# Low weight parts kept in DRAM between two blocks, and GpSimd's subtractions halved

## The chip, the cores and the metric

The kernel runs on one core of a Trainium2 chip. The metric is the device time of one execution in microseconds. Before the change three runs gave a median of 2254.72 us (2252.18 to 2258.6). Engines are named as in the profile: PE is TensorE's matmul, PEld its weight load, DVE is VectorE, ACT is ScalarE, POOL is GpSimd, SP issues DMAs.

## The reference

One layer of a hybrid decoder over 1024 prompt tokens and 64 decoded tokens, model width 2048. Everything is float32.

```python
h = rms_norm(x, p['norm_g'])
proj = h @ p['w_in']                      # 2048 x 6784
ps, g_a, u_b, g_b, u_c, v_c, g_c = jnp.split(proj, SPLIT_IDX, axis=-1)
y_a, new_shift, new_wkv = rwkv7_mix(ps, ...)   # 16 heads of 64, delta-rule state
y_b, new_pool = pool_mix(u_b, ...)             # trailing windows 2/4/8/16
y_c, vn_c = chunk_gate(u_c, v_c, ...)          # 128-position chunks
cat = jnp.concatenate([y_a * silu(g_a), y_b * silu(g_b), y_c * silu(g_c)], axis=-1)
out = x + cat @ p['w_out']                # 2048 x 2048
y = rms_norm(out, final_norm_g)
```

The two large products are what the change is about: each needs its weights, and the kernel computes each in float32 quality from pieces of lower precision.

## The kernel before, in words

The tokens go through in two blocks: block 0 is 512 prompt tokens and the 64 decoded ones, block 1 the other 512. Each block runs an in-projection (53 column tiles of 128 columns, in the order of `ORDER`) and then an out-projection. Both blocks read the whole of `w_in` and `w_out`.

A weight piece is 128 x 512 floats (256 KB). It is loaded by SP into `raw` (`wload`), rounded by ACT to the matmul type float32r as `whi` (`whigh`), and what the rounding lost is `wlo` = `raw` - `whi` (`wlow`). That subtraction stands on POOL for three pieces out of four and on DVE for the fourth (`wcount`, `V[6]`=4). A column tile has four pieces; a dense step (`dense_k`) makes three products: `whi` with the high activations (L237), `whi` with the low ones (L240), `wlo` with the high ones (L243). So each of the 212 pieces of `w_in` is loaded, rounded and subtracted twice, once in each block.

`Feed` says when that happens: while piece c is multiplied, step 1 rounds piece c+3, step 3 loads piece c+6, and step 0 (the last) subtracts piece c+3. There are 4 `raw`, 5 `whi` and 5 `wlo` buffers, so `whi` and `wlo` of piece c+5 take the places of piece c's.

Between the dense products run the side computations of the RWKV branch (`rwkv_unit`, 16 units a block, two for a pair of heads). They are generators: each `yield` names a number of ticks, a tick passes after a dense step, and what a generator emits is put into the program there. All engines execute in the order of the program as it is written (a manual schedule), so a PE instruction of a unit whose operands are late stops the dense products behind it. The places to follow are: the products of queries and keys `gp` (L680), which read `KG` and `BE`; `KG` is made by POOL (L664, L666) and by DVE (L558, a helper that all scalar_tensor_tensor instructions of DVE share); before these stand DVE's `kp` (L644), reciprocals (L640) and `BE` (L647); the recurrence over chunks (`cp` L871, copy to `W` by DVE and ACT L875 and L876, `cp` L883, copies to `SV` L885, `cq` L892, next `SV` by L558); and the inverse, whose product `d` (L823) reads `Q` (L836). POOL carries the inverse of 16 x 16 blocks (`Tu` L779, `Xu` L780) and, for the decoded rows of block 0, `svx` (L918). The unit's small transfers (`ndr`, `Nu`, `Xu`, `xd`, `X`) go through the same SP queue as the weights.

Of the kernel before, what the change touches and what calls it, by code (L numbers as in the profile page):

```python
# [9 lines left out]
F32 = mybir.dt.float32  # L10
F32R = mybir.dt.float32r
# [43 lines left out]
def tile_trunk(  # L55
# [21 lines left out]

    def ctile(shape, name, dt=F32):
        return const.tile(shape, dt, name=name)

    # ---------------------------------------------------------------- constants
# [26 lines left out]
    # ---------------------------------------------------------------- normalised inputs  # L108
    # the operand of a block's products, high and low parts, four feature tiles each
# [34 lines left out]
    # ---------------------------------------------------------------- dense pieces  # L144
    wcount = [0]

    def wload(src):
        raw = wp.tile([P, BLK + ND], F32, tag="raw", name="raw", bufs=4)
        sync.dma_start(raw[:, :512].rearrange("p (k c) -> p k c", c=src.shape[2]), src)
        return raw  # L150
# [6 lines left out]
    def wlow(raw, whi, eng=None, keep=None):  # L157
        wlo = keep[1] if keep else wp.tile([P, 512], F32R, tag="wlo", name="wlo", bufs=5)
        wcount[0] += 1
        eng = eng or (pool_e if wcount[0] % V[6] else dve)  # L160
        eng.tensor_sub(wlo, raw[:, :512], whi.bitcast(F32))  # L161
        return wlo

    def out_plan(b):
        # column group, feature tile, token tiles
        if b == 1:
            return [(g, k, range(4)) for g in range(4) for k in range(NK)]
        return [(g, k, range(5)) for g in range(3) for k in range(NK)] + [(3, k, t) for t in (range(2), range(2, 5)) for k in range(NK)]
# [8 lines left out]
    class Feed:  # L177
        # the weights' pieces in their order: loads run ahead of the splits, and those ahead of the products
        def __init__(self):
            self.src = [x for b in range(2) for x in [(ct, kh) for ct in ORDER for kh in range(4)] + out_plan(b)]  # L180
            self.raws, self.his, self.parts, self.keep, self.i = {}, {}, {}, {}, 0

# [8 lines left out]

        def low(self, i, eng=None):
            self.high(i)
            if i in self.raws and i not in self.parts:
                self.parts[i] = self.his[i], wlow(self.raws[i], self.his[i], eng, self.keep.get(i))

        def piece(self, ls):
            i = self.i
            for j in range(i, i + ls):
                self.low(j)  # L200
            self.i += 1
            return self.parts[i]

        def ahead(self, step):
            if step == V[3] % 4:
                self.high(self.i - 1 + LS)
            if step == V[4] % 4:
                self.low(self.i - 1 + LS)
            if step == V[5] % 4:
                j = self.i - 1 + LS + LD  # L210
                if len(self.src[j - 1]) == 2 or len(self.src[j - 2]) == 3:
                    self.load(j)

    # generators that go on beside the products, in ticks of those
# [33 lines left out]
    def dense(b, ct, hi, lo, feed, part=None):  # L248
        # part: the first half, where it is there already
        assert feed.src[feed.i] == (ct, 0)  # L250
        spans = ((0, UN), (UN, BLK + ND)) if b == 0 else ((0, BLK),)
        ps = [part or psd_tile()] + [psd_tile() for _ in spans[1:]]
        todo = list(zip(spans, ps))[1 if part else 0:]
        steps = 0
        for kh in range(4):
            piece = feed.piece(LS)
            for (t0, t1), q in todo:
                for k in range(4 * kh, 4 * kh + 4):
                    dense_k(q, hi, lo, k, piece, t0, t1, b == 1)
                    steps += 1  # L260
                    if steps < NK * len(todo):
                        tick()
                    if steps % len(todo) == 0:
                        feed.ahead(steps // len(todo) % 4)
        if b == 0:
            return [ps[0][:, :UN], ps[1][:, :UN + ND]]
        return [ps[0][:, :UN], ps[0][:, UN:]]
# [4 lines left out]
    with tc.tile_pool(name="prep", bufs=2) as pp, tc.tile_pool(name="setup", bufs=1) as sp, tc.manual_schedule():  # L272
        # the gain's row, spread over the partitions by the tensor engine
# [86 lines left out]
        def rescale(tt):  # L360
            # the scale of a tile as a diagonal, which its transposition multiplies by
            d = pp.tile([P, P], F32, name=f"dg{tt}", bufs=1)
            dve.tensor_scalar(d, ident, ss5[tt], None, op0=ALU.mult)
            return d
# [174 lines left out]
    # ---------------------------------------------------------------- RWKV branch  # L539
    def shift_evac(wk, b, ct, ps, xs, u):  # L540
        # token shift of half a column tile: (1 - mu) * now + mu * before
# [20 lines left out]
    def rwkv_unit(wk, b, p, u, lora, lw, got, pair_ops, zk):  # L562
        # yields the steps of the dense products to let pass before it goes on
# [29 lines left out]
        # decay, in-context rate, squared key norms  # L593
# [66 lines left out]
        # phase operands of a chunk and head, in the rows of the head: keys and queries;  # L660
        # in the other head's rows: their products with the chunk's keys
# [12 lines left out]
        # within-chunk products, masked to the past  # L674
# [25 lines left out]
        # X = (I - N)^-1: diagonal blocks of 16 by substitution, then blocks of 32 and 64  # L700
# [45 lines left out]
        # per head: the states, then the corrections, in the rows of the head, and the values in the others  # L746
# [29 lines left out]
        for r in range(1, 15):  # L776
# [4 lines left out]
            if dec and r == 7:  # L781
                # states of the decoded sequences
# [72 lines left out]
        # chunk recurrence  # L855
# [7 lines left out]
        # chunks one after the other; the decoded rows beside the first  # L863
# [42 lines left out]
        # group norm (token-major), bonus and gate (feature-major)  # L906
# [67 lines left out]
    # ---------------------------------------------------------------- pooling branch  # L974
# [34 lines left out]
    # ---------------------------------------------------------------- in-projection of a block  # L1009
    def in_block(wk, b, hi, lo, feed, part, raws):  # L1010
# [28 lines left out]
        def start(ps):  # L1039
# [12 lines left out]
            # stationary operands of both heads of a pair; the blocks between the heads stay zero  # L1052
# [67 lines left out]
        # spatial gating  # L1120
# [73 lines left out]
        def states():  # L1194
            # states that leave
# [49 lines left out]
    # ---------------------------------------------------------------- out-projection of a block  # L1245
    def cat_load(b, k):
        raw = wp.tile([P, BLK + ND], F32, tag="raw", name="raw", bufs=4)
# [8 lines left out]
    def first_cats(b, hi, lo, raws):  # L1256
        # the first rows of the out-projection, as soon as the last column tile has read what they overwrite
# [10 lines left out]
    def out_block(op, b, hi, lo, feed, raws):  # L1268
# [12 lines left out]
        if b == 0:  # L1281
            # the decoded rows: high and low parts side by side, so that two passes carry all their products
# [37 lines left out]
        def next_rows(j):  # L1320
            # a quarter of the next block's normalised inputs, feature-major
# [42 lines left out]
        def close(g, tt, q):  # L1364
# [15 lines left out]
            # the norm of a row's end  # L1380
# [29 lines left out]
        # the tiles of a group begin and end one after the other  # L1410
# [73 lines left out]
```

## Time and profile before

| quantity | value |
|---|---|
| median of 3 runs | 2254.72 us |
| profiled execution, first to last instruction | 2252.0 us |
| PE busy | 2163.5 us (96%) |
| PEld busy | 1860.5 us (83%) |
| DVE busy | 1212.4 us (54%) |
| POOL busy | 1066.7 us (47%) |
| ACT busy | 1006.0 us (45%) |
| DMA, mean | 98 GB/s, 221.18 MB |

The page gives the profiled execution by its span alone, 2252.0 us, which lies 2.7 us under the median of the runs. The table is read from the top: one engine is nearly always at work, and all others are idle half of the time. Such a table says little about the others' worth: what counts is where PE stands still, for how long, and which engine's instruction ended that. The windows of the profile cut the span into its stages: 60 to 960 us is block 0's in-projection, 960 to 1245 its out-projection, 1245 to 2060 block 1's in-projection, and the rest block 1's out-projection.

### The profile page before, as it was taken

The numbers are of one execution on the slowest core, as the hardware profiler recorded it, in microseconds if no ns is written. First come the engines' busy times: TensorE is split into PE (matmuls) and PEld (weight loads), VectorE is DVE, ScalarE is ACT, GpSimd is POOL, SyncE is SP. The second block draws the span as 40 slices with busy tenths as digits, with TensorE's granted clock in tenths as the row PEclk, the third lists the DMA queues.
The fourth block names the chain that finished last, engine by engine and source line by source line (L and its number), as shares of the span: only waits on it lengthen the run. The fifth ranks groups of instructions, "written<-read, shape, count | busy, mean of one in ns | idle before, by whom it ended". The sixth has DMA issues, their size and how long they took to land. (4 is left out here: it accounts for less than half of the span.)

```text
span 2252.0 us, 40898 instructions
## 1 busy us (share of the span) xinstructions
PE 2163.5 (96%) x14706; PEld 1860.5 (83%) x14706; DVE 1212.4 (54%) x2978; ACT 1006.0 (45%) x2680; POOL 1066.7 (47%) x1820
## 2 busy tenths in 40 slices
PE   7999999999999999999999999999999999999998
PEld 6998988988889899998887777777777778887786
DVE  6477677567667523214236467767676753323313
ACT  5344554554555442223334445555556454222323
POOL 5455555554555534223335455655555463432332
PEclk9999999999999999999999999999999999999999
DMA  5232232322222233336545432222222233334634
GB/s 153 77 75 64 75 78 58 76 72 65 74 70 70 74 87 96 93 95 195 175 150 178 129 81 77 74 72 77 75 73 78 72 85 95 95 116 129 191 122 140
DMA packets 390306, 221.18 MB, mean 98 GB/s; under 512 B 124054, under 2 KB 355736, under 8 KB 389207
## 3 DMA queue, kind: packets, MB, share of 16 engines
q1 hardware_dynamic: 390104, 218.58, 34.0%
q8 instruction: 116, 1.90, 0.4%
q14 instruction: 86, 0.70, 0.1%
HBM read 191.90 MB, written 26.61 MB: 97 GB/s over the span
## 5 line engine op out<-in xcount | busy, mean ns | idle before, releaser
L237 PE MATMUL dps<-a,whi 128*128 128x256 f32 (+1 forms) x2544 | 883.6, 347 | 2.1 <-ACT whi L154 1.9
L243 PE MATMUL dps<-a,wlo 128*128 128x256 f32 (+1 forms) x2544 | 844.5, 332 | 1.1 <-POOL wlo L161 0.7
L240 PE MATMUL dps<-a,whi 128*128 128x256 f32 (+1 forms) x2544 | 843.0, 331 | 0.0
L161 POOL TENSOR_TENSOR wlo<-raw,whi 128x512 fp32r<-128x512 f32 x415 | 550.5, 1330 | 591.2 <-ACT whi L154 541.7
L237 PEld LDWEIGHTS dps<-a,whi 128*128 128x128 f32 x2544 | 484.7, 191 | 48.9 <-issue 10.2
L243 PEld LDWEIGHTS dps<-a,wlo 128*128 128x128 f32 x2544 | 484.1, 190 | 33.5 <-POOL wlo L161 1.1
L240 PEld LDWEIGHTS dps<-a,whi 128*128 128x128 f32 x2544 | 485.5, 191 | 26.0 <-issue 0.2
L154 ACT CAST whi<-raw 128x512 fp32r<-128x512 f32 x552 | 338.6, 620 | 351.9 <-PE dps L240 117.4
L161 DVE TENSOR_TENSOR wlo<-raw,whi 128x512 fp32r<-128x512 f32 x137 | 101.8, 743 | 164.3 <-ACT whi L154 163.7
L1360 PE MATMUL ops<-whi,a 128*128 128x512 f32 x448 | 176.6, 394 | 2.5 <-ACT a L1253 1.8
L1361 PE MATMUL ops<-wlo,a 128*128 128x512 f32 x448 | 176.8, 395 | 2.2 <-POOL wlo L161 1.7
L1362 PE MATMUL ops<-whi,a 128*128 128x512 f32 x448 | 175.1, 391 | 0.1
L779 POOL TENSOR_TENSOR Tu<-Xu,Nu 32x14 f32<-32x14 f32 (+9 forms) x448 | 127.0, 283 | 27.3
L780 POOL TENSOR_TENSOR Xu<-Xu,Tu 32x14 f32<-32x14 f32 (+9 forms) x448 | 120.6, 269 | 35.1
L1361 PEld LDWEIGHTS ops<-wlo,a 128*128 128x128 f32 x448 | 84.1, 188 | 23.8 <-POOL wlo L161 5.6
L1360 PEld LDWEIGHTS ops<-whi,a 128*128 128x128 f32 x448 | 84.1, 188 | 22.0 <-ACT a L1253 2.3
L898 ACT ACTIVATE ZD<-SV,DC 64x64 f32<-64x64 f32 x192 | 66.2, 345 | 79.9 <-DVE SV L558 77.2
L1362 PEld LDWEIGHTS ops<-whi,a 128*128 128x128 f32 x448 | 84.1, 188 | 19.5 <-DVE a L1254 1.8
L922 POOL TENSOR_TENSOR sv<-sv,neghalf 128x4 f32<-128x4 f32 (+1 forms) x32 | 37.1, 1158 | 132.8 <-DVE sv L921 116.5
L871 PEld LDWEIGHTS cp<-SV,KG 128*128 128x128 f32 x544 | 77.5, 190 | 24.6 <-DVE SV L558 19.8
L871 PE MATMUL cp<-SV,KG 128*128 128x64 f32 x544 | 81.4, 271 | 9.6 <-DVE SV L558 9.6
L892 PEld LDWEIGHTS cq<-SV,Q 128*128 128x128 f32 x544 | 76.4, 190 | 15.3 <-DVE SV L885 11.0
(318 smaller groups left out, 3103.2 us busy)
## 6 DMA issues: line engine op xcount, KB each, us to landing
raw<-in_w_in_dram SPq DMA_DIRECT2D x424, 256.0 KB
raw<-in_w_out_dram SPq DMA_DIRECT2D x144, 256.0 KB
raw<-cat SPq DMA_DIRECT2D x32, 256.0 KB
res<-in_x_prompt_dram SPq DMA_DIRECT2D x32, 256.0 KB
out_dram<-res SPq DMA_DIRECT2D x32, 256.0 KB
x<-in_x_prompt_dram SPq DMA_DIRECT2D x4, 1024.0 KB
x<-in_x_prompt_dram SPq DMA_DIRECT2D x6, 512.0 KB
ndr<-N SPq DMA_DIRECT2D x48, 64.0 KB
```

Source lines behind the costliest of these rows:

```text
L154: act_e.copy(whi, raw[:, :512])
L161: eng.tensor_sub(wlo, raw[:, :512], whi.bitcast(F32))
L237: pe.matmul(o, lhsT=wh, rhs=xh, start=(k == 0), stop=False)
L240: pe.matmul(o, lhsT=wh, rhs=xl, start=False, stop=False)
L243: pe.matmul(o, lhsT=wl, rhs=xh, start=False, stop=(k == NK - 1))
L779: pool_e.tensor_tensor(tv, bc(Xu[:U, 0:r, r], 2, e), bc(Nu[:U, r, r + 1:16], 1, r), op=ALU.mult)
L780: pool_e.tensor_tensor(Xu[:U, 0:r, r + 1:16], Xu[:U, 0:r, r + 1:16], tv, op=ALU.add)
L871: pe.matmul(cw[i][:, h], lhsT=KG[:, q, h].rearrange("p a t -> p (a t)"), rhs=SV[:, q, h, :], start=True, stop=True)
L892: pe.matmul(cz[i][:, h], lhsT=Q2[:, q, h].rearrange("p a t -> p (a t)"), rhs=SV[:, q, h, :], start=True, stop=True)
L1360: pe.matmul(q, lhsT=ah, rhs=whi, start=(k == 0), stop=False)
L1361: pe.matmul(q, lhsT=ah, rhs=wlo, start=False, stop=False)
L1362: pe.matmul(q, lhsT=al, rhs=whi, start=False, stop=(k == NK - 1))
```

## The change

Two things are changed in the weights' path. Block 0 stores each `wlo` of `w_in`'s pieces 8 to 211 into a DRAM tile `wld` when the piece's products begin, and block 1 loads it from there and makes no subtraction for it; its `raw` is still loaded and rounded. In block 1 the load of `wlo`, and with it the rounding, of piece c+4 stands at step 3 of piece c, where before the rounding of piece c+4 stood at step 1 of piece c+1. And each subtraction that POOL still has is two instructions of 128 x 256 instead of one of 128 x 512. The `raw` buffers lose 64 unused columns. All other hunks of the diff only take out comments.

```diff
+    wld = drp.tile([DIN // P * 4, P, 512], F32, name="wld")
...
     def wload(src):
-        raw = wp.tile([P, BLK + ND], F32, tag="raw", name="raw", bufs=4)
+        raw = wp.tile([P, BLK], F32, tag="raw", name="raw", bufs=4)
...
         eng = eng or (pool_e if wcount[0] % V[6] else dve)
-        eng.tensor_sub(wlo, raw[:, :512], whi.bitcast(F32))
+
+        for c in ([slice(q * 256, (q + 1) * 256) for q in range(2)] if eng is pool_e else [slice(0, 512)]):
+            eng.tensor_sub(wlo[:, c], raw[:, c], whi[:, c].bitcast(F32))
         return wlo
...
             self.raws, self.his, self.parts, self.keep, self.i = {}, {}, {}, {}, 0
+
+            self.nin = 4 * len(ORDER)
+            self.n1 = self.nin + len(out_plan(0))
...
+        def cached(self, i):
+            return self.n1 + 8 <= i < self.n1 + self.nin
+
         def low(self, i, eng=None):
             self.high(i)
             if i in self.raws and i not in self.parts:
-                self.parts[i] = self.his[i], wlow(self.raws[i], self.his[i], eng, self.keep.get(i))
+                if self.cached(i):
+                    wlo = wp.tile([P, 512], F32R, tag="wlo", name="wlo", bufs=5)
+                    sync.dma_start(wlo.bitcast(F32), wld[i - self.n1])
+                else:
+                    wlo = wlow(self.raws[i], self.his[i], eng, self.keep.get(i))
+                self.parts[i] = self.his[i], wlo
...
             self.i += 1
+            if self.cached(i + self.n1):
+                sync.dma_start(wld[i], self.parts[i][1].bitcast(F32))
             return self.parts[i]
...
             if step == V[5] % 4:
+                if self.cached(self.i + LS):
+                    self.low(self.i + LS)
                 j = self.i - 1 + LS + LD
```

PE's instructions and their order stay as they were. On POOL the subtractions leave block 1's in-projection. Its program at the end of a unit's inverse in block 1 (`Tu`, `Xu`) up to the next unit's `KG`, before:

```order
L779 TENSOR_TENSOR Tu<-Xu,Nu 32x14
L780 TENSOR_TENSOR Xu<-Xu,Tu 32x14
L161 TENSOR_TENSOR wlo<-raw,whi 128x512 x2
L664 TENSOR_TENSOR KG<-xr,D 64x4x64 x2
L161 TENSOR_TENSOR wlo<-raw,whi 128x512
L719 TENSOR_TENSOR kpl<-kp,kph 128x256
L922 TENSOR_TENSOR sv<-sv,neghalf 128x4
L161 TENSOR_TENSOR wlo<-raw,whi 128x512
```

and now (line numbers are higher in the changed file, by 4 at the subtraction and by 19 in the unit):

```order
L798 TENSOR_TENSOR Tu<-Xu,Nu 32x14
L799 TENSOR_TENSOR Xu<-Xu,Tu 32x14
L683 TENSOR_TENSOR KG<-xr,D 64x4x64 x2
L738 TENSOR_TENSOR kpl<-kp,kph 128x256
L941 TENSOR_TENSOR sv<-sv,neghalf 128x4
```

Four `wlo` are gone from that stretch, and `KG` follows the inverse at once. DVE loses its quarter of the subtractions in the same stage. On POOL in block 0, from the decay's copies of a unit to the decoded rows' `svx`, before:

```order
L633 COPY DC<-D 128x4
L636 COPY DCd<-D 128x8
L161 TENSOR_TENSOR wlo<-raw,whi 128x512 x2
L664 TENSOR_TENSOR KG<-xr,D 64x4x64
L666 TENSOR_TENSOR KG<-xr,D 64x64
L664 TENSOR_TENSOR KG<-xr,D 64x4x64
L666 TENSOR_TENSOR KG<-xr,D 64x64
L161 TENSOR_TENSOR wlo<-raw,whi 128x512
L918 TENSOR_TENSOR svx<-SV,bm_89 128x512 x2
```

and now:

```order
L652 COPY DC<-D 128x4
L655 COPY DCd<-D 128x8
L165 TENSOR_TENSOR wlo<-raw,whi 128x256 x4
L683 TENSOR_TENSOR KG<-xr,D 64x4x64
L685 TENSOR_TENSOR KG<-xr,D 64x64
L683 TENSOR_TENSOR KG<-xr,D 64x4x64
L685 TENSOR_TENSOR KG<-xr,D 64x64
L165 TENSOR_TENSOR wlo<-raw,whi 128x256 x2
L937 TENSOR_TENSOR svx<-SV,bm_90 128x512 x2
```

Nothing moved there; each subtraction has become two. On SP in block 1, around a unit's first small transfers (`X` back from DRAM, then `ndr`), before:

```order
L806 DMA xd_79<-Xu 32x16x16
L149 DMA raw<-in_w_in_dram 128x4x128
L810 DMA X<-xd_79 64x4x64 x2
L149 DMA raw<-in_w_in_dram 128x4x128 x2
L724 DMA ndr<-N 64x4x64 x2
L149 DMA raw<-in_w_in_dram 128x4x128
L744 DMA Nu<-ndr 32x16x16
```

and now:

```order
L825 DMA xd_79<-Xu 32x16x16
L207 DMA wlo<-wld 128x512
L151 DMA raw<-in_w_in_dram 128x4x128
L829 DMA X<-xd_79 64x4x64 x2
L207 DMA wlo<-wld 128x512
L151 DMA raw<-in_w_in_dram 128x4x128
L207 DMA wlo<-wld 128x512
L151 DMA raw<-in_w_in_dram 128x4x128
L743 DMA ndr<-N 64x4x64 x2
L207 DMA wlo<-wld 128x512
L151 DMA raw<-in_w_in_dram 128x4x128
L763 DMA Nu<-ndr 32x16x16
```

A load of `wlo` stands in front of every load of `raw`, and the unit's transfers keep their places among them.

## Rows read from the trace of the kernel before

**Rows 1.** Windows by stage: length, busy time by engine, clock, DMA share, GB/s.
```profile
60.00:960.00 900.00, 873.13 (x7422) 820.70 (x7421) 522.48 (x1421) 406.60 (x1168) 448.45 (x836) 0.98 0.28 75
960.00:1245.00 285.00, 281.52 (x1427) 237.02 (x1426) 113.44 (x148) 107.96 (x206) 103.89 (x89) 1.00 0.50 158
1245.00:2060.00 815.00, 780.60 (x4814) 618.02 (x4813) 482.74 (x1244) 394.55 (x1120) 416.15 (x776) 1.00 0.31 86
```

**Rows 2.** Waits of PE, block 1's in-projection: total us, times, longest.
```profile
PE gp L680 <- DVE KG L558: 12.9, 17, 3.0
PE cp L883 <- ACT yc L880: 7.0, 7, 1.1
PE cp L871 <- DVE SV L558: 5.2, 13, 0.4
```

**Rows 3.** Timeline of DVE near 1418 us: start, us, instruction.
```profile
1417.94 1.56 DVE L644 TENSOR_TENSOR kp<-kp,xk 128x256 f32<-128x256 f32 x1
...
1420.35 0.21 DVE L875 COPY W<-cp 64x64 f32<-64x64 f32 x1
```

**Rows 4.** Timeline of POOL, same stretch.
```profile
1417.94 1.28 POOL L161 TENSOR_TENSOR wlo<-raw,whi 128x512 fp32r<-128x512 f32 x1
```

**Rows 5.** Timeline of PE, same stretch; in brackets its idle time before.
```profile
1421.18 0.43 PE L883 MATMUL cp<-W,XB 128*128 128x64 f32 x2 [1.10 <-ACT yc L880]
```

**Rows 6.** Groups by line and shape, 1245 to 2060 us: busy us, mean ns, idle before.
```profile
L161 POOL TENSOR_TENSOR wlo<-raw,whi 128x512 fp32r<-128x512 f32 x157 | 206.2, 1316 | 151.6 <-ACT whi L154 138.1 <-PE mp L1101 4.1 <-DVE BE L558 3.8
...
L161 DVE TENSOR_TENSOR wlo<-raw,whi 128x512 fp32r<-128x512 f32 x52 | 41.5, 798 | 33.8 <-ACT whi L154 33.6
...
L644 DVE TENSOR_TENSOR kp<-kp,xk 128x256 f32<-128x256 f32 x16 | 15.2, 950 | 2.5 <-ACT kp L631 2.1
...
L719 POOL TENSOR_TENSOR kpl<-kp,kph 128x256 fp32r<-128x256 f32 x16 | 12.1, 754 | 23.5 <-ACT kph L716 22.9
...
L967 DVE TENSOR_TENSOR bv<-yf,bv 128x256 f32<-128x256 f32 x16 | 6.8, 426 | 36.6 <-ACT yf L963 36.6
```

**Rows 7.** Waits of PE, block 0's in-projection.
```profile
PE d L823 <- DVE Q L836: 8.9, 7, 1.4
PE cp L871 <- DVE SV L558: 4.3, 7, 0.8
PE cq L892 <- DVE SV L885: 3.8, 7, 0.6
```

**Rows 8.** Timeline of DVE near 380 us.
```profile
379.01 2.05 DVE L558 SCALAR_TENSOR_TENSOR BE<-xk,der,Di 64x320 f32<-64x320 f32 x2
...
381.35 1.88 DVE L558 SCALAR_TENSOR_TENSOR KG<-xk,der,D 64x256 f32<-64x256 f32 x2
```

**Rows 9.** Timeline of POOL, same stretch.
```profile
379.21 1.50 POOL L161 TENSOR_TENSOR wlo<-raw,whi 128x512 fp32r<-128x512 f32 x1 [0.99 <-POOL KG L666]
380.68 2.47 POOL L918 TENSOR_TENSOR svx<-SV,bm 128x512 f32<-128x512 f32 x2
```

**Rows 10.** Timeline of PE, same stretch.
```profile
381.37 0.68 PE L892 MATMUL cq<-SV,Q 128*128 128x64 f32 x4 [0.59 <-DVE SV L885]
383.49 0.65 PE L823 MATMUL d<-Q,X 64*64 64x32 f32 x16 [1.44 <-DVE Q L836]
```

**Rows 11.** Windows at a granted clock of 0.50, columns as in Rows 1.
```profile
299.25:302.66 3.41, 3.41 (x18) 2.65 (x16) 3.23 (x15) 1.66 (x6) 0.02 (x1) 0.50 0.00 0
384.58:388.00 3.42, 3.42 (x16) 3.27 (x15) 3.24 (x14) 0.74 (x3) 0.00 (x0) 0.50 0.02 5
...
736.16:742.98 6.82, 6.82 (x27) 4.10 (x28) 5.16 (x16) 1.34 (x3) 2.41 (x2) 0.50 0.10 23
1289.12:1292.53 3.41, 3.41 (x14) 2.25 (x13) 0.14 (x2) 1.51 (x4) 1.97 (x2) 0.50 0.00 0
```

**Rows 12.** Groups by line and shape, 60 to 960 us.
```profile
L161 POOL TENSOR_TENSOR wlo<-raw,whi 128x512 fp32r<-128x512 f32 x144 | 191.6, 1333 | 181.2 <-ACT whi L154 152.2 <-DVE BE L558 14.2 <-POOL KG L666 6.7
```

**Rows 13.** Waits of ACT, block 0's out-projection.
```profile
ACT whi L154 <- DMA raw<-in_w_out_dram: 27.6, 17, 4.8
```

More of the change, by code (lines that the diff above doesn't have):

```diff
@@ L1246, in cat_load @@
     def cat_load(b, k):
-        raw = wp.tile([P, BLK + ND], F32, tag="raw", name="raw", bufs=4)
+        raw = wp.tile([P, BLK], F32, tag="raw", name="raw", bufs=4)
         sync.dma_start(raw[:, :BLK], catd[b][k, :, :BLK])
```

## Prediction

> **What bounds the kernel now.** I read the windows by stage first [rows 1]. In block 0's in-projection PE is at work for 873.1 of 900 us, in block 1's for 780.6 of 815; the idle time is 26.9 and 34.4 us. In the out-projection between them it is 3.5 us. DVE and POOL are busy for about half of each stage. PE's instructions and their order are the same in both kernels, so the change can give no more than PE's idle time and what a low clock costs, and it gives even that only where a late operand is earlier.
>
> Then the waits of PE by stage. In block 1 most end with DVE's `KG` (12.9 us), the copies that `cp` at L883 needs (7.0) and DVE's next state `SV` (5.2) [rows 2]. In block 0 they end with DVE's `Q` (8.9), `SV` (4.3) and the copy L885 (3.8), seven times each, so once a pair of heads [rows 7].
>
> Then a stretch before such a wait, engine by engine. At 1417.94 DVE's `kp` and POOL's `wlo` start together; `wlo` takes 1.28 us and `kp` 1.56 [rows 3, 4]. The product of the same size in L967 takes 0.426 us, and `kp` in the mean 0.950 [rows 6]. So DVE's instruction of two SBUF operands stood until POOL's was over. The copy to `W`, queued behind it on DVE, started at 1420.35, and PE stood 1.10 us at L883 [rows 3, 5]. Here is the price of the subtraction: not its own time, but what it holds up on DVE.
>
> Last the granted clock. It is at 0.50, the lower of the two levels (1.2 of 2.4 GHz), in six stretches of block 0 (three of 3.4 us, three of 6.8, first and last shown) and in two of 3.4 us in block 1 [rows 11]. PE had stood still shortly before: 0.59 and 1.44 us around 382, and the clock is low from 384.58 [rows 10, 11]. At half speed 30.7 us of block 0 lose at most 15.4 us, 6.8 us of block 1 lose 3.4.
>
> **The change part by part.** *Block 1 without subtractions.* DVE and POOL lose nearly all of 52 subtractions at 798 ns (41.5 us) and 157 at 1316 ns (206.2 us) [rows 6]. With POOL's goes the hold. DVE's line in front of `gp` is a run of instructions such as `kp` and `BE`, each with two SBUF operands, and `KG` now follows the inverse on POOL at once. One hold costs up to 1.1 us (1.56 less 0.43), and most single waits at `gp` and L883 are no longer than that. I count the waits at `gp` as gone (12.9), those at L883 (7.0) too, half of those for `SV` (2.6), since a recurrence has its own length, and a third of the 9.3 us that is left of the 34.4 (3.1): 25.6 us. With the waits before them gone, so are the two slow stretches: 3.4. Sum 29 us. Bounds: 0 and 37.8 (34.4 and 3.4); below zero by rival 3.
>
> *Halves in block 0.* A half is not in the trace of before, but POOL's `kpl` is the same subtraction at 128x256: 754 ns [rows 6]. Two are 1508 ns against 1333, so 144 of them cost POOL 25 us more [rows 12]. POOL is idle for half of the stage, which hides it; uncovered it would be 25 us. What it buys: a held DVE instruction waits for at most 0.75 us in place of 1.3. At 379 POOL's `wlo` runs beside the two `BE`, which take 2.05 us, then two `svx` (2.47 us) beside two `KG` of DVE (1.88 us) [rows 8, 9]. Of the short waits for `SV` and L885, 0.6 us each, I count two thirds as gone: 5.4 of 8.1 us. The wait at `d` keeps its `svx`, which is not halved; a third of 8.9 goes: 3. The clock: shorter waits should spare some low stretches, not all; 6 of 15.4 us. Less 2 us for where the longer POOL queue shows: 12 us. Bounds: a gain of 42 (26.9 and 15.4) and a loss of 25.
>
> The Trainium skill ("SBUF — State Buffer", Who interferes with whom) says that whichever of the two engines issues first holds the shared ports for the whole instruction, and that issue order decides which one blocks. The held `kp` agrees on the first half of that. On the second half it speaks against halving: a second half already queued on POOL could be first again. Rival 1 works that out.
>
> *Stores in block 0.* 204 transfers of 256 KB on SP's queue. A store stands behind the load of `raw` for five pieces later, which itself waited for a later subtraction, so it waits for nothing new. A subtraction into a `wlo` place waits for the place's store, but also, as before, for PE to be done with the piece, and the store is issued when that piece's products begin. Cost nothing; the cover is the length of a piece's products (900 us over 212 pieces, 4.2 us).
>
> *Loads in block 1.* 204 more of 256 KB. The out-projection moves 158 GB/s at a share of 0.50 [rows 1], so a transfer of 0.262 MB takes 0.83 us of all 16 engines; 204 take 170 us, and the share in this stage goes from 0.31 to 0.52, which the out-projection bears with 3.5 us of idle PE. The load waits for PE to finish piece c-1, at step 3 of piece c; what is behind it on SP (the unit's `ndr`, `X`, `Nu`, `Xu`) is written later in the program still, so it would not have had its data sooner. From there to the use are more than three pieces (815 us over 212, 3.8 us each), against a few us of transfer. Cost nothing.
>
> *Rounding one step earlier, two pieces after its load.* ACT's rounding now waits for PE to begin piece c, so ACT keeps a lead of three quarters of a piece. Cost nothing while `raw` lands within two pieces (7.7 us); otherwise rival 3.
>
> *Out-projections.* POOL's subtractions are halved there too; PE's idle time is 3.5 us in block 0's. I count nothing.
>
> **Sum.** 2252.0 - 29 - 12 = 2211 us for the profiled execution. That one lies 2.7 us under the median of the runs, so 2214 us.
>
> **Rivals.** *1. The halves buy nothing: POOL's second half takes the ports before DVE does.* The evidence against: two `svx` stand one behind the other on POOL, and the first of DVE's two `KG` got through between them, for both took 1.88 us while the two `svx` took 2.47 [rows 8, 9]. For: `svx` is another shape, and halves have nothing at all between them. Block 1 gives its 29, block 0 loses 2: 2252 - 29 + 2 + 2.7 = 2228.
>
> *2. No change: PE meets the next late operand.* Chains whose start does not hang on the removed wait do not move with PE. If block 1 gives 15 in place of 29 because copies of ACT and DVE are late as soon as DVE is not, and block 0's POOL shows half of its extra 25 us: 2252 - 15 + 12 + 2.7 = 2252. For it: waits of 0.6 us at seven places look like the length of a chain. Against: the same instruction at 0.43 and 1.56 us.
>
> *3. Slower: ACT waits for `raw`.* Loads now have two pieces before they are read, with twice the weight bytes queued. In the out-projection, where loads are also two pieces ahead, ACT waited 27.6 us for them, in 17 waits, over 80 pieces [rows 13], 0.35 us a piece. At 204 pieces that is 70 us of ACT, which stands in line for the copies to `W` and `SV`. If all of it reaches PE: 2252 - 41 + 70 + 2.7 = 2284. It decides from the point where more than 41 of the 70 arrive. Against: a piece of block 1 is longer than one of the out-projection (3.8 against 3.6 us), and PE's waits in the out-projection were few in spite of it [rows 1].
>
> The Trainium skill ("DMA: Bandwidth & Descriptors", Issuing engines are not separate DMA queues) says that all transfers run on the same 16 engines and interleave. By that the new loads stand in front of the unit's small transfers. No run here shows yet what that delays.
>
> **How the numbers follow.** Forecast 0.69, rival 1 0.16, rival 2 0.09, rival 3 0.06. The forecast's own range is 2191 to 2233 (block 1 gives 20 to 36, block 0 gives 2 to 28). The range of 8 in 10 takes in rival 1 and reaches half-way from there to rival 2: 2193 to 2243. A difference under 0.3% (6.8 us) can't be told from no change here. Faster: nearly all of the forecast (0.68), rival 1 (0.15) and a third of rival 2 (0.03), 0.86. Slower: rival 3 (0.05) and a little of rival 2, 0.06. The same: 0.08.
>
> **What would show it.** In block 1's window PE's idle time falls from 34 to about 9 us, `kp` (now L663) has a mean near 0.43 us, the DMA share is about 0.5, no stretch there has the clock at 0.50. In block 0 PE idles about 18 us and fewer stretches are slow; POOL's half takes about 0.75 us. Wrong would be: ACT's rounding waiting for `raw` in block 1 by more than 40 us, DVE's held instructions in block 0 as long as before, or PE's waits in block 1 back under other names.

## The result, and the profile after

The changed kernel takes 2218.03 us (median of 4 runs, 2213.85 to 2220.11); the kernel before, run beside it, 2253.59 (4 runs, 2252.18 to 2258.6). The ratio is 0.9845, with a 95% interval of 0.9818 to 0.9872: 35.6 us faster, against 41 forecast. The profiled execution went from 2252.0 to 2218.4 us.

Where the time went is read first by stage. The stages are cut here at PE's first product of each, so that a stage's length is what the kernel spends in it; [rows 1] were cut at round times, and their window of the out-projection holds 65 us of the in-projections on either side. Before, cut this way (length, busy time by engine, clock, DMA share, GB/s; block 0's in-projection, its out-projection, block 1's in-projection, its out-projection):

```profile
34.20:1017.70 983.50, 955.57 (x8044) 901.28 (x8043) 552.48 (x1500) 433.32 (x1222) 481.86 (x891) 0.98 0.29 77
1017.70:1237.40 219.70, 216.22 (x961) 173.43 (x961) 93.75 (x107) 88.15 (x167) 85.54 (x74) 1.00 0.56 176
1237.40:2063.60 826.20, 791.79 (x4865) 627.29 (x4864) 490.72 (x1260) 401.78 (x1134) 420.77 (x781) 1.00 0.31 86
2063.60:2243.00 179.40, 177.36 (x769) 143.51 (x767) 52.44 (x72) 58.88 (x112) 60.95 (x48) 1.00 0.47 150
```

After:

```profile
33.40:1003.20 969.80, 949.66 (x8043) 898.80 (x8042) 539.66 (x1500) 433.49 (x1222) 515.14 (x1053) 0.99 0.44 133
1003.20:1228.40 225.20, 219.12 (x961) 175.47 (x960) 82.98 (x106) 88.06 (x167) 108.96 (x135) 0.98 0.56 176
1228.40:2026.30 797.90, 786.63 (x4864) 624.66 (x4863) 411.23 (x1209) 401.97 (x1134) 211.83 (x634) 1.00 0.56 156
2026.30:2209.40 183.10, 179.44 (x769) 144.46 (x767) 45.73 (x72) 58.94 (x112) 71.51 (x94) 0.99 0.46 149
```

Block 1's in-projection is 28.3 us shorter, block 0's 13.7; the two out-projections are longer, by 5.5 and 3.7. PE's idle time (length less PE's busy time) fell from 34.4 to 11.3 us in block 1 and from 27.9 to 20.1 in block 0. The granted clock stood at 0.50 for 30.7, 0, 6.8 and 0 us of the four stages before, and for 27.3, 6.8, 0 and 3.4 us after. In block 1 POOL's busy time halved (420.8 to 211.8) and the DMA share rose from 0.31 to 0.56.

The waits of PE in block 1's in-projection (total us, times, longest) answer to [rows 2]:

```profile
PE cq L911 <- DVE SV L904: 4.0, 10, 0.9
PE cp L902 <- ACT yc L899: 2.3, 7, 0.4
...
PE dps L256 <- ACT whi L156: 1.4, 1, 1.4
PE gp L699 <- DVE KG L577: 1.0, 2, 0.6
```

`gp` for `KG` went from 12.9 us to 1.0, the copies that `cp` needs (L902, L883 before) from 7.0 to 2.3, the state `SV` at the first `cp` from 5.2 to nothing in the list. One wait is new: `cq` for the copy to `SV`, 4.0 us. In block 0, answering to [rows 7], only this is left of the three:

```profile
PE d L842 <- DVE Q L855: 7.1, 7, 1.1
```

One wait has grown there, at the start of the stage: `xps` for DVE's `x` near 38 us, 3.0 us where it was 0.8. It takes 2.6 to 3.0 us in every changed version, with the stores or without, and its cause stays open.

The cause, DVE's held instruction, is seen in its mean (line, shape, count, busy us, mean ns; block 1, then block 0). `kp` took 950 ns in block 1 [rows 6], 487 now; in block 0, where POOL still subtracts but in halves, eight of them took 1200 ns before and 621 now. Block 0 before:

```profile
L644 DVE TENSOR_TENSOR kp<-kp,xk 128x256 f32<-128x256 f32 x8 | 9.6, 1200 | 1.0 <-ACT kp L631 1.0
```

Block 1 and block 0 after:

```profile
L663 DVE TENSOR_TENSOR kp<-kp,xk 128x256 f32<-128x256 f32 x16 | 7.8, 487 | 6.5 <-ACT kp L650 5.4
...
L663 DVE TENSOR_TENSOR kp<-kp,xk 128x256 f32<-128x256 f32 x8 | 5.0, 621 | 1.0 <-ACT kp L650 1.0
```

Not every group got shorter: the other eight `kp` of block 0, 128 x 320, went from 672 to 797 ns. The six groups on 128 partitions that make `kp` and `BE` in block 0 took 38.5 us together and take 29.0 now. POOL's half itself takes 788 ns in the mean, two of them 1576 where one whole took 1333 [rows 12]:

```profile
L165 POOL TENSOR_TENSOR wlo<-raw,whi 128x256 fp32r<-128x256 f32 x324 | 248.0, 788 | 221.2 <-ACT whi L156 186.8 <-issue 19.1 <-POOL KG L685 7.5
```

The stretch near 380 us, engine by engine, as in [rows 8 to 10]. DVE:

```profile
379.79 1.50 DVE L577 SCALAR_TENSOR_TENSOR BE<-xk,der,Di 64x320 f32<-64x320 f32 x2
381.32 0.22 DVE L904 COPY SV<-cp 64x64 f32<-64x64 f32 x1
381.57 1.57 DVE L577 SCALAR_TENSOR_TENSOR KG<-xk,der,D 64x256 f32<-64x256 f32 x2
383.06 0.27 DVE L855 TENSOR_TENSOR Q<-qa,maskA 128x128 f32<-128x128 f32 x1
```

POOL:

```profile
379.99 1.89 POOL L165 TENSOR_TENSOR wlo<-raw,whi 128x256 fp32r<-128x256 f32 x2 [0.99 <-POOL KG L685]
381.84 2.22 POOL L937 TENSOR_TENSOR svx<-SV,bm 128x512 f32<-128x512 f32 x2
```

PE:

```profile
381.59 0.67 PE L911 MATMUL cq<-SV,Q 128*128 128x64 f32 x4
383.39 0.65 PE L842 MATMUL d<-Q,X 64*64 64x32 f32 x16 [1.13 <-DVE Q L855]
```

The two `BE` take 1.50 us where they took 2.05: DVE gets through between the halves, which stretches them to 1.89 us together. Taken one by one, the second `BE` runs from 380.35 to 381.29, past the start of the second half (380.90), which then takes 0.98 us. The copy to `SV` behind `BE` is in time, and `cq`, which waited 0.59 us, waits no longer. Two `svx`, not halved, still stand beside `KG`, and `d` still waits, 1.13 us where it was 1.44.

### The profile page after: what moved, and what is told of

It reads as the page before. It is cut to its first block, busy times and chain, and to the rows that moved or that the text cites. A ratio compares the mean times of both kernels' runs of the same rounds, so it can differ in the third digit from the quotient of the medians.

```text
span 2218.4 us, 41676 instructions
## 1 busy us (share of the span) xinstructions
PE 2157.3 (97%) x14706; PEld 1858.2 (84%) x14706; DVE 1102.6 (50%) x2927; ACT 1006.4 (45%) x2680; POOL 924.9 (42%) x1941
## 5 line engine op out<-in xcount | busy, mean ns | idle before, releaser
L165 POOL TENSOR_TENSOR wlo<-raw,whi 128x256 fp32r<-128x256 f32 x524 | 413.3, 812 | 511.6 <-ACT whi L156 380.8
L799 POOL TENSOR_TENSOR Xu<-Xu,Tu 32x14 f32<-32x14 f32 (+9 forms) x448 | 125.4, 280 | 35.1
L165 DVE TENSOR_TENSOR wlo<-raw,whi 128x512 fp32r<-128x512 f32 x86 | 61.8, 718 | 152.8 <-ACT whi L156 152.3
L798 POOL TENSOR_TENSOR Tu<-Xu,Nu 32x14 f32<-32x14 f32 (+9 forms) x448 | 118.2, 264 | 29.2
L556 DVE SCALAR_TENSOR_TENSOR sl<-sl,dps 128x256 f32<-128x256 f32 x64 | 27.9, 438 | 125.7 <-ACT sl L555 125.7
L890 PEld LDWEIGHTS cp<-SV,KG 128*128 128x128 f32 x544 | 77.3, 190 | 11.3 <-DVE SV L577 6.4
```

The source lines that it names most:

```text
L165: eng.tensor_sub(wlo[:, c], raw[:, c], whi[:, c].bitcast(F32))
L798: pool_e.tensor_tensor(tv, bc(Xu[:U, 0:r, r], 2, e), bc(Nu[:U, r, r + 1:16], 1, r), op=ALU.mult)
L799: pool_e.tensor_tensor(Xu[:U, 0:r, r + 1:16], Xu[:U, 0:r, r + 1:16], tv, op=ALU.add)
L890: pe.matmul(cw[i][:, h], lhsT=KG[:, q, h].rearrange("p a t -> p (a t)"), rhs=SV[:, q, h, :], start=True, stop=True)
```

## The experiments

The theory: what the subtraction cost was the hold, POOL's instruction keeping DVE's two-operand instructions waiting, and time is gained whether it is shortened (block 0) or taken away (block 1). The rivals: that it is the time of POOL or of DVE that was freed, that PE waited for `wlo` itself, that one part of the change does all. Where two stage lengths are compared, PE's idle time and the time at a clock of 0.50 in the stage are given beside them if they change the reading; half of that time is the most that the low clock can have cost. The diffs are against the changed kernel; stage lengths are cut as above, in the order block 0 in, out, block 1 in, out.

**The loads alone: all subtractions that are left are whole again.**

```diff
-        for c in ([slice(q * 256, (q + 1) * 256) for q in range(2)] if eng is pool_e else [slice(0, 512)]):
+        for c in [slice(0, 512)]:
```

> The loads and stores of the low parts alone; all subtractions that POOL still has are whole (128 x 512). If the two edits act apart (hold theory: a subtraction on POOL costs PE only by holding DVE's two-operand instructions), block 1's in-projection takes the 798 us of the changed kernel, block 0's is back at 983 us, which also shows the stores at no cost, the out-projections are back at 220 and 179 us, and the whole is about 2225 us. If the stores cost something that the halves hid, block 0 is above 986 us. If the gain in block 1 needed the halves, it is above 805 us.

Measured: 2229.19 us (2222.88 to 2233.98), ratio to before 0.9906 (0.9876 to 0.9936). Stages 980.2, 220.5, 799.8, 178.3. Block 1 has the whole gain of the change (799.8 against 797.9), block 0 none that shows (980.2 against 983.5), though the stores are in it, and its waits of [rows 7] are as before: 8.9, 4.2 and 3.9 us. So block 0's gain is not theirs. That they cost nothing is not to be read from this length, for the clock was at 0.50 for 13.7 us of it, against 30.7 before; the next version is the better test. The out-projections are as short as before.

**The halves alone: nothing is loaded, block 1 subtracts as before.**

```diff
-            return self.n1 + 8 <= i < self.n1 + self.nin
+            return False
```

> Halves everywhere, no loads or stores of low parts. Hold theory: block 0 takes 970 us as in the changed kernel; block 1, where POOL now holds DVE for at most 0.75 us at a time, falls from 826 to about 808 us; the out-projections stay at 225 and 183 us; the whole about 2230 us. If block 0's gain came from elsewhere (addresses, the smaller buffer, the stores' pace), block 0 is above 978 us. If holds add up whatever their length, block 1 stays at 820 us or more.

Measured: 2226.5 us (2225.36 to 2230.03), ratio 0.989 (0.9865 to 0.9914). Stages 967.5, 221.7, 811.7, 183.1. Block 0 has its gain without stores (967.5 us and 19.5 us of idle PE, against 969.8 and 20.1 with them), and block 1 gets half of what the loads give (811.7 between 826.2 and 797.9). By PE's idle time it gets more, 14.6 us (34.4 to 19.8) of the 23.1; the clock was at 0.50 for 13.7 us there, 6.8 before. The first out-projection was expected to stay at 225 us and took 221.7. POOL is busier than ever in block 1:

```profile
1224.10:2035.80 811.70, 791.89 (x4865) 629.67 (x4864) 473.36 (x1260) 401.82 (x1134) 453.11 (x940) 0.99 0.32 87
```

POOL works 453.1 us where it worked 420.8, and the stage is shorter: it was not POOL's time.

**Which engine's subtraction: DVE makes its own quarter of block 1 again, POOL's three quarters are loaded.**

```diff
-            return self.n1 + 8 <= i < self.n1 + self.nin
+            return self.n1 + 8 <= i < self.n1 + self.nin and (i - self.n1) % 4 != 3
...
-                    wlo = wlow(self.raws[i], self.his[i], eng, self.keep.get(i))
+                    kept = self.n1 + 8 <= i < self.n1 + self.nin
+                    wlo = wlow(self.raws[i], self.his[i], dve if kept else eng, self.keep.get(i))
+                    wcount[0] -= kept
```

> In block 1 only POOL's three of four low parts are loaded; DVE makes its 51 subtractions as before. Hold theory: POOL's subtractions were the price, so block 1's in-projection takes 800 to 804 us against 798 with all loaded and 826 before. Rival, DVE's time: the 41.5 us of DVE's own subtractions were what made KG late; then block 1 is at 815 us or more.

Measured in one run: 2212.99 us. Stages 969.4, 224.1, 793.1, 181.7.

```profile
1227.60:2020.80 793.20, 782.83 (x4865) 625.07 (x4864) 445.84 (x1260) 400.29 (x1134) 218.98 (x634) 1.00 0.49 140
```

DVE works 34.6 us more than in the changed kernel, and the stage is 4.7 us shorter, not longer: freeing DVE of its quarter bought nothing. The new wait of `cq` for `SV`, 4.0 us above, is 0.7 here, and 0.7 again in the version further on that keeps DVE's quarter too. Why the fourth load brings that wait was not tried.

**And the other way round: DVE's quarter is loaded, POOL makes its three quarters, whole.**

```diff
...
-            return self.n1 + 8 <= i < self.n1 + self.nin
+            return self.n1 + 8 <= i < self.n1 + self.nin and (i - self.n1) % 4 == 3
...
-                    wlo = wlow(self.raws[i], self.his[i], eng, self.keep.get(i))
+                    kept = self.n1 + 8 <= i < self.n1 + self.nin
+                    wlo = wlow(self.raws[i], self.his[i], pool_e if kept else eng, self.keep.get(i), kept)
+                    wcount[0] -= kept
```

(with the last argument `wlow` makes one instruction.)

> In block 1 only DVE's quarter of the low parts is loaded; POOL makes its 153 subtractions, whole. Hold theory: block 1's in-projection is near before, 818 us or more of 826. Rival, DVE's time: it is under 808 us.

Measured in one run: 2242.8 us. Stages 964.7, 221.0, 829.6, 182.9. Block 1 is as long as before, with 33.2 us of idle PE (34.4 before). All of its gain hangs on POOL's subtractions.

**POOL reads: the changed kernel, and POOL subtracts as it did, into `raw`, whose value nobody reads any more.**

```diff
                 self.low(self.i - 1 + LS)
+                d = self.i - 1 + LS
+                if self.cached(d) and (d - self.n1) % 4 != 3:
+                    pool_e.tensor_sub(self.raws[d], self.raws[d], self.his[d].bitcast(F32))
```

> The changed kernel, and in block 1's in-projection POOL makes the three of four subtractions again, whole, at the place where they stood, into the raw buffer, where nobody reads the result. Hold theory: most of the 28 us of block 1 comes back, 798 to 815 us or more, with L663 (kp) at 0.8 us or more in the mean, although PE waits for none of the results. If what was gained was the wait of PE for the result, or DVE's own subtractions, block 1 stays under 803 us.

**POOL only writes: in the same place three `memset` of 128 x 384 into `raw`.**

```diff
+                    for _ in range(3):
+                        pool_e.memset(self.raws[d][:, :384], 0.0)
```

> As the run with the subtractions that nobody reads, but three memsets of 128 x 384 in the place of each, so POOL is as long at work (about 1.3 us a piece) and reads no SBUF. Hold theory: memsets do not hold DVE, block 1 stays at 798 to 803 us and L663 near 0.43 us. Rival, POOL's time: what counted was that POOL is busy and its KG and inverse come later; then block 1 is as long as with the subtractions, 815 us or more.

Measured, one run each: reading 2257.1 us, stages 968.2, 224.6, 838.0, 182.1; writing 2219.43 us, stages 968.9, 222.0, 798.8, 185.1. POOL's group and the window of block 1, reading:

```profile
L228 POOL TENSOR_TENSOR raw<-raw,whi 128x512 f32<-128x512 f32 x153 | 199.3, 1308 | 100.8 <-ACT whi L156 88.4 <-POOL raw L228 4.8 <-issue 4.2
```
```profile
1226.40:2064.30 837.90, 800.14 (x4863) 631.29 (x4862) 452.04 (x1209) 402.14 (x1134) 408.94 (x787) 0.99 0.53 149
```

writing:

```profile
L229 POOL MEMSET raw<- 128x384 f32 x459 | 191.2, 420 | 106.1 <-ACT whi L156 86.5
```
```profile
1224.70:2023.50 798.80, 787.19 (x4864) 624.84 (x4863) 411.11 (x1209) 402.12 (x1134) 400.71 (x1091) 1.00 0.56 156
```

The same engine is busy for the same time (408.9 and 400.7 us) at the same places, nobody needs what it makes, and one version is 39 us slower in block 1 than the other. PE idles for 37.8 us beside the reader and for 11.6 beside the writer; the clock is at 0.50 for 23.9 us and for none, at most 12 of the 39. What PE waits for longest beside the reader is DVE:

```profile
PE cq L914 <- DVE SV L907: 16.3, 23, 1.4
PE gp L702 <- DVE KG L580: 9.2, 14, 3.3
```

and beside the writer:

```profile
PE cq L915 <- DVE SV L908: 4.1, 10, 0.9
...
PE gp L703 <- DVE KG L581: 0.6, 1, 0.6
```

DVE's 1209 instructions take 452.0 us beside the reader and 411.1 beside the writer, against 411.2 in the changed kernel. The hold fell on another instruction than in the kernel before: `kp` has a mean of 614 ns, but the `BE` behind it, 400 ns in the changed kernel, has this:

```profile
L669 DVE TENSOR_TENSOR BE<-kp,Di 128x256 f32<-128x256 f32 x16 | 19.6, 1224 | 0.0
```

So it is not POOL's time that costs but its instruction, through DVE. Reading is not all that parts the two: a `memset` is also shorter than a subtraction (420 against 1308 ns). But short subtractions cost too. DVE's instructions other than its own subtractions take 448.4 us in block 1 before, 431.6 with the halves alone (774 ns each) and 409.3 in the changed kernel, so halves cost DVE 22 of the 39 us, and the writer (409.1) costs it nothing. That speaks for the reading. The Trainium skill ("SBUF — State Buffer", Who interferes with whom) says that a DVE instruction with two SBUF inputs contends with a GpSimd instruction that reads SBUF, and not with one that only writes it. These two runs agree with both halves.

**The third rival's wait: every load of `wlo` is followed on SP's queue by a copy of the same 256 KB from DRAM to DRAM.** All copies go to one tile, so each waits for the one before to land.

```diff
+    wlx = drp.tile([P, 512], F32, name="wlx")
...
                     sync.dma_start(wlo.bitcast(F32), wld[i - self.n1])
+                    sync.dma_start(wlx, wld[i - self.n1])
```

> The changed kernel with a further 256 KB copy from DRAM to DRAM behind each load of a low part, read by nobody, so that the DMA share of block 1's in-projection goes from 0.56 to about 0.8. If the transfers are covered with room to spare (the prediction's cost of nothing), block 1 stays within 3 us of 798. If they are near the point of the third rival (ACT waits for raw), ACT's rounding waits for raw by more than 40 us and block 1 is above 810 us.

Measured in one run: 2255.08 us, block 1's in-projection 830.4, its DMA share 0.73 and 214 GB/s. ACT's waits for `raw`, and PE's for `wlo`, there:

```profile
ACT whi L157 <- DMA raw<-in_w_in_dram: 136.4, 54, 7.0
```
```profile
PE dps L264 <- DMA wlo<-wld: 13.0, 18, 1.6
```

The whole gain of the loads is lost again. But SP waited 138.0 us for landings of `wlx` in this stage, so bytes and the held queue are both in this. The next kernel tells them apart.

**The same copies, each to a place of its own.**

```diff
+    wlx = drp.tile([DIN // P * 4, P, 512], F32, name="wlx")
...
+                    sync.dma_start(wlx[i - self.n1], wld[i - self.n1])
```

> The further 256 KB copy from DRAM to DRAM again, each into a place of its own, so that no copy waits for the one before it to land. If the 32 us that the copy cost in block 1's in-projection came from SP standing in the wait for the earlier copy (138 us of SP's waits), block 1 is back under 803 us. If they came from the transfers themselves (bytes and packets in the same queue, ACT's rounding late by raw), it stays above 815 us with ACT waiting for raw by 80 us or more.

Measured in one run: 2223.7 us, block 1's in-projection 802.7, DMA share 0.73 and 222 GB/s.

```profile
ACT whi L157 <- DMA raw<-in_w_in_dram: 77.7, 35, 6.6
```

SP waited 1.1 us for `wlx` in the whole run. The same bytes at the same share cost 4.8 us (802.7 against 797.9); the queue that stands still for a landing cost the other 28. And 77.7 us of ACT waiting for `raw` reach PE as 5 at most: ACT had the time.

**Whole subtractions in the out-projections, halves elsewhere.**

```diff
...
-        for c in ([slice(q * 256, (q + 1) * 256) for q in range(2)] if eng is pool_e else [slice(0, 512)]):
+        for c in ([slice(q * 256, (q + 1) * 256) for q in range(2)] if eng is pool_e and not whole else [slice(0, 512)]):
...
-                    wlo = wlow(self.raws[i], self.his[i], eng, self.keep.get(i))
+                    wlo = wlow(self.raws[i], self.his[i], eng, self.keep.get(i), len(self.src[i]) == 3)
```

> The changed kernel with whole subtractions in the two out-projections, halves in block 0's in-projection alone. If the 9 us that the out-projections lost (5.5 and 3.7) come from the halves, which DVE's runs of two-operand instructions keep waiting one by one, they are back at 220 and 179 us, and the whole is about 2209 us. If they come from the stores or from the memory layout, they stay at 225 and 183 us.

Measured: 2212.22 us (5 runs, 2207.93 to 2218.14), ratio 0.9814 (0.9791 to 0.9837), which overlaps with the changed kernel's 0.9818 to 0.9872. Stages 968.6, 221.7, 797.5, 180.8: the out-projections give 3.5 and 2.3 us back. Over all kernels of this study, the second out-projection is 181.7 us or longer in the eight with halves in it (the changed one, 183.1; 190.9 in the one whose queue was held) and 177.5 to 180.8 in the five with whole instructions; the first overlaps (221.0 to 225.2 against 219.7 to 221.7). The time of a run goes with its mean granted clock, so runs at the same clock compare better than medians: at 0.990 this version took 2218.14 us and the changed kernel 2220.11, at 0.993 2213.11 and 2210.69 against 2217.17, at 0.994 2207.93 against 2213.85. By that whole instructions there are worth 2 to 6 us.

**What the study points to, together:** whole instructions in the out-projections, DVE's quarter of block 1 made and not loaded, and `svx` halved.

```diff
-                pool_e.tensor_tensor(svx[:, h], bc(SV[:, 4, h, :], 1, NB), bc(bm8, 2, 64), op=ALU.mult)
+                for q in (slice(0, 4), slice(4, 8)):
+                    pool_e.tensor_tensor(svx[:, h, q], bc(SV[:, 4, h, :], 1, 4), bc(bm8[:, q], 2, 64), op=ALU.mult)
```

(and the edits of the two versions named)

> Three edits on the changed kernel: whole subtractions in the out-projections, DVE's quarter of block 1's subtractions made by DVE again (no store or load for them), and the decoded rows' svx of block 0 in four instructions in place of two. If they add up: the out-projections at about 221 and 181 us, block 1 at 793 us, and block 0 at about 963 us against 969, because the wait at d (7.1 us, behind svx) falls below 4 us; the whole about 2202 us. If svx in quarters buys nothing, block 0 stays at 968 us or more.

Measured: 2201.02 us (5 runs, 2199.55 to 2206.44), ratio to before 0.9769 (0.9749 to 0.9789), outside the changed kernel's interval and below it: this one beats both. Stages 962.0, 220.4, 796.1, 177.5. PE's wait in block 0, with `svx` in halves, goes from 7.1 to

```profile
PE d L844 <- DVE Q L857: 4.6, 7, 0.7
```

It is the same reading as before: a long POOL instruction of two operands beside DVE's `KG`. The stage is the shortest of all, but not all of its 7.8 us below the changed kernel come from `svx`. The clock is at 0.50 for 17.1 us there, against 27.3, which is up to 5.1 us; PE's idle time fell by 4.0 (20.1 to 16.1). The version with POOL's subtractions kept in block 1 has `svx` whole and the same 17.1 us, and its block 0 takes 964.7. At the same mean clock the whole kernel is 13 us below the changed one (at 0.990, 2206.44 against 2220.11; at 0.994, 2200.87 to 2201.25 against 2213.85).

**The kernel before, once more, to see what one profile's stages are worth.**

> The kernel before, profiled a second time, to see how far its stages repeat: block 0's in-projection 983 us and block 1's 826 us, each within 5 us, with the granted clock at half speed in other places but for a similar total (30.7 and 6.8 us).

Measured in one run: 2253.31 us; stages 981.5, 220.8, 826.3, 180.3, against 983.5, 219.7, 826.2, 179.4. So a difference of 2 us in a stage of one profile says nothing, and block 1's 28 or block 0's 13 do. The time at a clock of 0.50 was 30.7 us in block 0 and 6.8 in block 1 in the one profile, 27.3 and 10.2 in the other: it moves between runs of one kernel. It moves a stage by more than 2 us, too: in the thirteen profiles block 0 has the low clock for 13.7 to 30.7 us. The runs of the kernel before go with it, from 2243.12 us at a mean clock of 0.997 to 2257.43 at 0.987.

## Why the prediction was right, and where its terms were off

*Block 1, 29 us.* Right in size, 28.3, and in mechanism. Idle time gave 23.1 (25.6 predicted) and no stretch there has the low clock any more (6.8 us before, so 3.4, as predicted; the other profile of the kernel before had 10.2, so the size is luck to within 2 us); the 1.8 that is left is in neither row. By line, with the start of each of PE's instructions compared between the two traces (they are the same and in the same order), `gp` gave 15.4 us, L871 8.0 and L883 6.1, and `cq` took 4.8 back. Rival 2 had other waits come up; that one did. What the readers and writers on POOL showed in addition: not the engine's freed time but its reading was the price. The 41.5 us of DVE's own subtractions, taken away with POOL's, were worth nothing.

*Block 0, 12 us.* Right as a sum, 13.7, but not by its parts, so the agreement is partly luck. The waits for `SV` and L885 were counted at 5.4; by the starts they gave 9.7 (L871 5.9, `cq` 3.8), all of what they had cost and more. Not counted either way were the product `bp` (L758), which gave 2.7, and the wait of `xps` at the start, which cost 2.5. `d` gave 2.0 of the 3 counted. The clock was counted at 6, and 30.7 us at 0.50 became 27.3, which is 1.7 and no more than what two runs of the kernel before differ by. POOL's longer queue, counted at 2, does not show: the 33 us more of POOL's work (515.1 against 481.9) fell into its idle time.

*Out-projections, nothing.* This is the term that was mis-sized: they lost 9.2 us, which is more than the whole miss (the profiled execution was forecast at 2211 us and took 2218). By PE's idle time they lost 4.3 (3.5 to 6.1, and 2.0 to 3.7); the rest goes with the low clock, which they have for 10.2 us and had for none, at most 5.1. The argument was that PE idled for 3.5 us only, which bounds what can be gained and says nothing of what can be lost. Who comes next when both wait was weighed for DVE's held instructions alone (rival 1), and here it is POOL that is held. POOL near 1165 us in the changed kernel, single instructions:

```profile
1164.35 0.73 POOL L165 TENSOR_TENSOR wlo<-raw,whi 128x256 fp32r<-128x256 f32 x1 [0.57 <-ACT whi L156]
...
1166.19 3.58 POOL L165 TENSOR_TENSOR wlo<-raw,whi 128x256 fp32r<-128x256 f32 x1
1169.73 1.17 POOL L165 TENSOR_TENSOR wlo<-raw,whi 128x256 fp32r<-128x256 f32 x1
```

DVE there:

```profile
1164.39 2.98 DVE L1351 TENSOR_TENSOR res<-res,fg 128x512 f32<-128x512 f32 x3
1167.30 0.67 DVE L165 TENSOR_TENSOR wlo<-raw,whi 128x512 fp32r<-128x512 f32 x1
1167.91 3.53 DVE L1351 TENSOR_TENSOR res<-res,fg 128x512 f32<-128x512 f32 x4
```

PE, and the window of the low clock that follows:

```profile
1170.95 0.50 PE L1380 MATMUL ops<-wlo,a 128*128 128x512 f32 x1 [2.98 <-POOL wlo L165]
```
```profile
1172.11:1175.52 3.41, 3.41 (x10) 2.66 (x9) 0.00 (x0) 1.09 (x2) 2.55 (x4) 0.50 0.83 260
```

A half that takes 0.73 us took 3.58 beside a run of DVE instructions of two operands (eight from 1164.39 to 1171.44); four of these, at 0.67 or 0.68 us each, ran while it waited. The second half of its piece came at 1170.90, PE stood 2.98 us for it, and the clock fell at 1172.11. The same half took 3.57 or 3.58 us in four other versions (DVE's quarter kept, the reader, both copies), each time with a wait of PE of 3.0 us and a low stretch that begins within 1.5 us of the wait's end. In the other three versions with halves there it did not come, and that stage has no low stretch; whole instructions took 1.83 us there at most in four versions and 2.52 in the fifth. In the first out-projection such halves have a mean of 890 ns (788 in block 0). Two halves in place of one whole give DVE shorter holds, and give POOL one more place at which it can be kept waiting. Where POOL's result is needed at once, as here, that is the wrong way round. That the whole instructions gave back 5.8 us fits this; by runs at the same clock it is 2 to 6, so its size stays open by a few us.

*Stores, loads, rounding, nothing.* Held. With halves, block 0 takes 967.5 us without stores and 969.8 with them, and PE idles for 19.5 and 20.1 us. The loads raised the share to 0.56, where 0.52 was worked out, and ACT's waits for `raw` of `w_in` in block 1 came to this:

```profile
ACT whi L156 <- DMA raw<-in_w_in_dram: 13.4, 8, 7.0
```

13.4 us where rival 3 would have had 70. Against making DVE's quarter on DVE, loading it costs some 2 to 5 us (797.9 against 793.1 and 796.1).

*The rivals.* The first is refuted: with halves block 0 takes 962 to 970 us in every kernel, without them 980 to 984 in three profiles; PE's idle time there is 16 to 20 us with them and 28 to 31 without. The rule of the Trainium skill from which it was drawn ("SBUF — State Buffer", Who interferes with whom: issue order decides who blocks) leaves open who is next when both wait. The rows near 380 us show DVE getting in between two halves, those near 1166 us a run of DVE getting in before POOL. The second too: one new wait of 4 us, not 14. The third's chain is real, but its price was taken at one for one: 77.7 us of ACT's waiting reached PE as 5. Where the queue waits for a landing the loads' whole gain is lost (830.4), but by another chain: PE waits for `wlo` itself (13.0 us), and of ACT's waiting one wait of 5.2 us (`n2p` for `sqh`) is new. The rival's 3.6 us for a piece of the out-projection came from the window that holds 65 us of other stages; cut at PE's first products it is 2.7 (219.7 over 80), which speaks more strongly against the rival than was said. Half-way from rival 1 to rival 2 is 2240, not the 2243 of the wider range; nothing hangs on that. What the prediction left open, what the new transfers delay as they interleave with the small ones, was not taken apart; a second set of as many bytes costs 5 us.

## What to carry to other kernels

Price a helper engine's instruction by what it holds up: look for a two-operand DVE instruction that runs far over its solo time beside it, in front of a product. Shortening the holder takes most of that away without moving any work (half of block 1's gain by length and two thirds by PE's idle time, all of block 0's), but only where its own result has slack; leave it whole where the matmul is next in line for it. And a small idle time bounds what a stage can gain, never what it can lose.

## What was not expected of the hardware

A DVE instruction gets in between two POOL instructions that are queued back to back (two `BE` at 1.50 us in place of 2.05, the halves at 1.89 together), and so does a whole run of DVE against one waiting POOL instruction: 3.58 us for a half. POOL writing 459 `memset` cost DVE nothing (411.1 against 411.2 us); POOL reading cost it 41 us. A DMA issue that waits for an earlier landing costs the queue behind it 28 us, where the same bytes unhindered cost 5. And the time at the low clock did not shrink with PE's idle time: outside the last 9 us it was 37.5 us before and 37.5 after (30.7 and 6.8 in the in-projections, then 27.3 there and 6.8 and 3.4 in the out-projections). Over all profiles it goes from 13.7 us (the loads alone, PE idle for 49) to 54.6 (the reader, idle for 68), and what sets it stays open.
